# The second block of a top-2 expert folds its halves into its own accumulator banks, and its down products run by pairs of weight pieces

## The chip, the cores and the metric

One core of a Trainium2 chip runs the whole kernel as one launch. The metric is the device time of one execution in microseconds (us). The engines are TensorE (PE in the profile, with PEld for its weight loads), VectorE (DVE), ScalarE (ACT), GpSimd (POOL) and SyncE (SP), which issues most DMAs. Differences of under about 0.3% can't be told from none on this kernel.

## The reference

The layer takes x of 2048 tokens by 1024 channels. A mixer (windowed attention, a bidirectional mLSTM, two merge gates) adds to x; then a mixture of experts adds to it again:

```
h = rmsnorm(x, norm2_g)
group  = argmax(h @ w_rg + b_rg)                    # one of 4
top2   = top_k(expert logits of that group, 2)      # of 8 experts
weight = softmax(top2 values) * p_group
for each expert e (32 of them), for the tokens routed to it:
    y = (silu(xb @ w_gate[e]) * (xb @ w_up[e])) @ w_down[e]     # 1024 -> 512 -> 1024, float32
    out[token] += weight * y
```

The expert weights are 6.3 MB per expert in float32, all of which are read. The change lies in the experts alone.

## The kernel before, in words

Up to about 1744 us of the span the kernel runs the mixer and the router; from there to the end it runs a loop over the 32 experts. Every float32 operand of a large product is kept as a high and a low part in the engine's faster float32 form (`ehi`/`elo` for weights, `xhi`/`xlo` for tokens, `hhi`/`hlo` for the hidden layer), and a product is three or four matmuls of 128 rows by 512 columns.

Weights come by DMA from SP into a ring of six tiles (`raw`, `rawd`). `wsplit` cuts each tile into two pieces; ScalarE writes a piece's high part (L1572), VectorE its low part (L1573). An expert has 12 pieces: 0 to 7 for gate and up, 8 to 11 for down. The pieces of the next expert are split at named places of the present one, from a fixed table (`SPLITS`).

The tokens of an expert are handled in blocks. Block A (class `Block`) takes the first 128. Where an expert has between 129 and 192 tokens, a second block B (class `Small`) takes up to 64 more. It lays the high parts of its 64 tokens and their low parts side by side as the 128 stationary columns, so one matmul per weight part does for both (L1710); the two 64-row halves of the sum have to be added afterwards. The number of tokens is known only at run time, so B's work stands in `tc.If(v > 0)`, with A's part of the same stretch in both branches. In this data 15 of the 32 experts have a block B.

All of this stage is issued in the written order (a manual schedule), and each engine runs its own instructions in that order. The order on TensorE for an expert with a block B is:

1. A's gate and up products (L1619, L1622); B's transposes (L1704), the rest of A's, and B's gate and up products into two PSUM banks, `self.ps[0]` and `self.ps[1]` (L1710). ScalarE copies the first bank to `g[:, 0]` (L1718), VectorE the second to `g[:, 1]` (L1720).
2. `A_.after`: A's down products for pieces 0 and 1, then the transposes of A's second hidden half into A's tile `th` (`A_.p`, one PSUM bank; L1638). ScalarE reads them into `hhi` (L1639) and VectorE into `hlo` (L1640). At the place `t1` the first weight pieces of the next expert are split and its tokens transposed (`xturn`, L1596, read by L1597 and L1598).
3. `A_.end(between)`: `between(0)`, A's down products of pieces 2 and 3 for the left half (L1647, L1650), `between(1)`, the same for the right half. `between(h)` is `B_.fold(h, A_.p)`.
4. `B_.down`: B's 16 down matmuls into `self.ps[0]` and `self.ps[1]` (L1710), whose two halves ScalarE and VectorE then add with the token's weight (L1741, L1742). GpSimd adds the result to the output in DRAM (L1744).

`fold(h)` turns the 128 rows of `g[:, h]` into columns and adds the two halves in one step, with a matmul against `sel`, which holds two 64 by 64 identities on top of each other (L1726). Four such products, two matmul records each, give a 128 by 256 result in PSUM: for h = 0 in the first half of A's bank `th`, for h = 1 in its second half. Then ScalarE takes the silu of half of it (L1728), VectorE multiplies by the other half (L1729, the last read of that bank), ScalarE writes the high part (L1731) and VectorE the low part (L1732) of `hs`, the stationary operand of B's down products: fold 0 makes `hs[:, 0:2]`, fold 1 makes `hs[:, 2:4]`.

The framework places the waits. It takes two uses of the same PSUM bank as one another's to wait for, whichever columns they touch. The scopes that matter:

```
A_ = Block(...)     # th: mp.tile([P, 2, 2, P], F32, name="th"), one buffer
B_ = Small(...)     # self.ps: two banks, tags a0B and a1B
```

Of the kernel before, what the change touches and what calls it, by code (L numbers as in the profile page):

```python
# [102 lines left out]
def body(tc, A, out, scr_ext=None, upto="all"):  # L103
    nc = tc.nc
    scr_ext = scr_ext or {}
    es = ExitStack()
    with es:
        pass
        _body(tc, nc, A, out, scr_ext, upto, es)


def _body(tc, nc, A, out, scr_ext, upto, es):
# [875 lines left out]
    while pi < len(plan) and plan[pi][1] not in ("br", "wo"):  # L988
        c, kind, i = plan[pi]
# [339 lines left out]
    def put(si, ent, i, n):  # L1329
        for u in range(n):  # L1330
            nc.gpsimd.indirect_dma_start(
                out=slot_ap, out_offset=bass.IndirectOffsetOnAxis(ap=si[:, i, u:u + 1], axis=0),
                in_=ent[:, i, u, :], in_offset=None)
# [85 lines left out]
    while pi < len(plan):  # L1419
        c, kind, i = plan[pi]  # L1420
# [13 lines left out]
        if kind == "wo" and i == 0:  # L1434
            for u in range(TPC):
                t = c * TPC + u
# [139 lines left out]
    def wsplit(n):  # L1576
        if n >= NPC * N_EXP or n in wts:
            return
        wload(n // 2)
        wts[n] = split(raws[n // 2], n % NPC)  # L1580
        if n % 2:
            del raws[n // 2]
            wload(n // 2 + NRAW)

    def gather(col, tag):
        xg = mo.tile([P, D], F32, name="xg", tag="xg" + tag, bufs=2)
        nc.gpsimd.indirect_dma_start(out=xg, out_offset=None, in_=h2_ap,
                                     in_offset=bass.IndirectOffsetOnAxis(ap=col, axis=0))
        return xg

    def xturn(xg, i):

        xs = [mo.tile([P, 4, P], F32R, name=f"x{m}{i}") for m in ("hi", "lo")]
        p = mp.tile([P, 4, P], F32, name="tr", bufs=2)
        for k in range(4):
            nc.tensor.transpose(p[:, k, :], xg[:, (4 * i + k) * P:(4 * i + k + 1) * P], ident)  # L1596
        nc.scalar.activation(xs[0], p, AF.Copy)  # L1597
        nc.vector.tensor_sub(xs[1], p, xs[0].bitcast(F32))  # L1598
        return xs

    class Block:
# [40 lines left out]
        def down(self, h, ks):  # L1642
            if len(self.dn) == h:
                self.dn.append(self.ps())
            for k in ks:
                for w_ in self.wt(8 + k):
                    nc.tensor.matmul(self.dn[h], self.hhi[:, k, :], w_[:, h, :],  # L1647
                                     start=k == 0 and w_ is self.wt(8)[0], stop=False)
            for k in ks:
                nc.tensor.matmul(self.dn[h], self.hlo[:, k, :], self.wt(8 + k)[0][:, h, :], start=False, stop=k == 3)  # L1650
# [39 lines left out]
    class Small:  # L1690
# [28 lines left out]
                else:  # L1719
                    nc.vector.tensor_copy(self.g[:, 1, :], self.ps[1])  # L1720

        def fold(self, h, room):

            p = room[:, h].rearrange("p a (b t) -> p (a b) t", b=2)
            for k in range(4):
                nc.tensor.matmul(p[:, k, :], self.g[:, h, k * P:(k + 1) * P], sel, start=True, stop=True)  # L1726
            a = self.a[:, h]
            nc.scalar.activation(a, p[:, 0:2], AF.Silu)  # L1728
            nc.vector.tensor_mul(a, a, p[:, 2:4])  # L1729
            hs = self.hs[:, 2 * h:2 * h + 2]  # L1730
            nc.scalar.activation(hs[:, :, 0, :], a, AF.Copy)  # L1731
            nc.vector.tensor_sub(hs[:, :, 1, :], a, hs[:, :, 0, :].bitcast(F32))  # L1732

        def down(self):
            y = self.g[0:64].rearrange("p h f -> p (h f)")
            for k in range(4):
                for h in range(2):
                    self.product(h, self.hs, self.wt(8 + k), k, 4)
            for h in range(2):
                cs = slice(512 * h, 512 * h + 512)  # L1740
                nc.scalar.activation(y[:, cs], self.ps[h][64:128, :], AF.Copy, scale=self.wgt[64:128, :])  # L1741
                nc.vector.scalar_tensor_tensor(y[:, cs], self.ps[h][0:64, :], self.wgt[0:64, :], y[:, cs],  # L1742
                                               op0=OP.mult, op1=OP.add)
            nc.gpsimd.indirect_dma_start(out=out, out_offset=bass.IndirectOffsetOnAxis(ap=self.idx[0:64, :], axis=0),  # L1744
                                         in_=y, in_offset=None, compute_op=OP.add)
# [10 lines left out]
    def gather_small(e):  # L1756

        t = mo.tile([P, D], F32, name="xgB")
        nc.gpsimd.indirect_dma_start(out=t[0:64, :], out_offset=None, in_=h2_ap,
                                     in_offset=bass.IndirectOffsetOnAxis(ap=idx[0:64, 32 + e:33 + e], axis=0))  # L1760
        return t
# [20 lines left out]
    for e in range(N_EXP):  # L1782
        v = nc.values_load(two[:, e:e + 1], min_val=0, max_val=1)
        w_e = lambda k, e=e: wts[NPC * e + k]
        xsN = []

        def at(place):
            if place == "a1":
                if e + 1 < N_EXP:
                    xgB[e + 1] = gather_small(e + 1)  # L1790
                if e + 2 < N_EXP:
                    xg[e + 2] = gather(idx[:, e + 2:e + 3], "")
            if place == "d1" and held:
                put(*held.pop(0))
            for j in SPLITS.get(place, ()):
                wsplit(NPC * e + j)
            if place == "t1" and e + 1 < N_EXP:
                xsN.extend(xturn(xg[e + 1], i) for i in range(2))

        A_ = Block(w_e, xsA, idx[:, e:e + 1], wgt[:, e:e + 1])  # L1800
        B_ = Small(w_e, xgB[e], idx[:, 32 + e:33 + e], wg2[:, e:e + 1])
        A_.begin(at)
        with tc.If(v > 0) as cmp:
            B_.turn()
            A_.middle()
            B_.up()
        with cmp.Else():
            A_.middle()
        A_.after(at)
        with tc.If(v > 0) as cmp:  # L1810
            A_.end(lambda i: B_.fold(i, A_.p))
            B_.down()
        with cmp.Else():
            A_.end()
        at("end")
        xsA = xsN
# [44 lines left out]
```

## Time and profile before

| | |
|---|---|
| median of 3 runs | 2579.93 us (2575.63 to 2582.38) |
| profiled execution: its own time | 2579.44 us |
| its span, first to last instruction | 2577.6 us |
| granted TensorE clock, mean over the span | 0.977 of full speed |
| busy: PE, PEld, DVE, ACT, POOL | 94%, 81%, 64%, 51%, 36% |
| block B's: copies to g (L1718, L1720), folds | 15 of each copy, 30 folds |
| DMA | 515 MB, 200 GB/s in the mean |

The expert stage is the last 830 us or so of the span, the last 13 of the 40 slices of the page. A matmul record has a modelled end, and neighbouring matmuls overlap in it by design, so distances between starts are the safer measure.

### The profile page before, as it was taken

How to read it: one execution, taken by the hardware profiler on the slowest of the kernel's cores; microseconds unless marked ns; L12 is line 12 of the kernel's file. 1: busy time of each engine (PE TensorE's matmuls, PEld its weight loads, DVE VectorE, ACT ScalarE, POOL GpSimd, SP SyncE). 2: the span in 40 equal slices, each digit the busy share in tenths (PEclk: the TensorE clock that was granted, in tenths of full speed). 3: DMA queues.
4: the chain of work that ended last, by engine and by line, in shares of the span. 5: the costliest groups of instructions: out<-in, count | busy, mean ns of one | idle time of the engine just before them, and what ended most of it. 6: DMA issues, size and time to landing. Idle time of an engine off the chain costs nothing. (4 is left out here: it accounts for less than half of the span.)

```text
span 2577.6 us, 39210 instructions
## 1 busy us (share of the span) xinstructions
PE 2420.9 (94%) x13932; PEld 2090.1 (81%) x13933; DVE 1660.2 (64%) x2795; ACT 1312.2 (51%) x2564; POOL 931.0 (36%) x918
## 2 busy tenths in 40 slices
PE   7999999999999999997898889979999999999997
PEld 6889988899889989886787778867777777777776
DVE  4465455664556655578659484677866776778665
ACT  4455455464556555454342333236755665667554
POOL 5543444443543533333444445432221222122111
PEclk9999999999999999998999999989999999999999
DMA  4535434453445445556867565459998897889974
GB/s 146 162 116 169 148 109 125 144 181 94 127 138 158 134 121 163 182 174 193 244 193 209 176 180 168 131 192 322 363 318 294 255 328 235 299 255 361 343 245 103
DMA packets 348413, 515.33 MB, mean 200 GB/s; under 512 B 25019, under 2 KB 212500, under 8 KB 348188
## 3 DMA queue, kind: packets, MB, share of 16 engines
q1 hardware_dynamic: 332140, 460.03, 54.4%
q0 software_dynamic: 14880, 48.20, 8.0%
q10 hardware_dynamic: 1168, 4.21, 0.4%
q8 instruction: 127, 2.08, 0.3%
q14 instruction: 98, 0.80, 0.1%
HBM read 420.83 MB, written 91.54 MB: 199 GB/s over the span
## 5 line engine op out<-in xcount | busy, mean ns | idle before, releaser
L239 POOL TENSOR_TENSOR wlo<-wraw,whi 128x512 fp32r<-128x512 f32 (+1 forms) x422 | 574.1, 1390 | 403.2 <-ACT whi L236 386.4
L1573 DVE TENSOR_TENSOR elo<-raw,ehi 128x1024 fp32r<-128x1024 f32 x256 | 299.4, 1219 | 27.5 <-ACT ehi L1572 27.4
L319 PE MATMUL mm<-hThi,whi 128*128 128x512 f32 x768 | 306.4, 399 | 0.0
L319 PE MATMUL mm<-hTlo,whi 128*128 128x512 f32 x768 | 304.9, 397 | 0.0
L319 PE MATMUL mm<-hThi,wlo 128*128 128x512 f32 x768 | 303.6, 395 | 0.0
L236 ACT ACTIVATE whi<-wraw 128x512 fp32r<-128x512 f32 (+1 forms) x424 | 234.0, 622 | 130.0 <-PE mm L319 75.9
L319 PE MATMUL mm<-whi,hThi 128*128 128x256 f32 (+1 forms) x896 | 262.1, 292 | 3.0 <-ACT ev L908 1.8
L1572 ACT ACTIVATE ehi<-raw 128x1024 fp32r<-128x1024 f32 x256 | 254.1, 1050 | 19.7 <-DMA raw<-w_expert_up 17.8
L319 PE MATMUL mm<-wlo,hThi 128*128 128x256 f32 (+1 forms) x896 | 257.5, 287 | 1.5 <-POOL wlo L239 1.5
L319 PE MATMUL mm<-whi,hTlo 128*128 128x256 f32 (+1 forms) x896 | 258.1, 288 | 0.0
L1687 POOL DMA_INDIRECT out<-y,idx x32 | 55.4, 1731 | 448.8 <-DVE y L1686 223.2
L1619 PE MATMUL mm<-ehi,xhi 128*128 128x512 f32 x512 | 205.5, 401 | 0.0
L1619 PE MATMUL mm<-ehi,xlo 128*128 128x512 f32 x512 | 201.0, 393 | 0.4 <-DVE xlo L1598 0.4
L319 PEld LDWEIGHTS mm<-whi,hThi 128*128 128x128 f32 x896 | 172.3, 192 | 5.4 <-ACT ev L908 2.1
L319 PEld LDWEIGHTS mm<-wlo,hThi 128*128 128x128 f32 x896 | 172.4, 192 | 2.5 <-POOL wlo L239 1.8
L319 PEld LDWEIGHTS mm<-whi,hTlo 128*128 128x128 f32 x896 | 171.9, 192 | 0.9 <-DVE hTlo L449 0.2
L319 PEld LDWEIGHTS mm<-hThi,wlo 128*128 128x128 f32 x768 | 144.4, 188 | 31.1
L319 PEld LDWEIGHTS mm<-hThi,whi 128*128 128x128 f32 x768 | 144.6, 188 | 29.1
L319 PEld LDWEIGHTS mm<-hTlo,whi 128*128 128x128 f32 x768 | 144.5, 188 | 28.3
L1622 PE MATMUL mm<-elo,xhi 128*128 128x512 f32 x512 | 159.0, 392 | 0.0
L1573 DVE TENSOR_TENSOR elo<-rawd,ehi 128x1024 fp32r<-128x1024 f32 x128 | 151.4, 1220 | 11.6 <-ACT ehi L1572 11.4
L833 DVE SCALAR_TENSOR_TENSOR cacc<-cstg,colv,cacc 128x512 f32<-128x512 f32 x128 | 108.1, 845 | 58.4 <-ACT cacc L830 56.5
(456 smaller groups left out, 5932.0 us busy)
## 6 DMA issues: line engine op xcount, KB each, us to landing
wraw<-w_in SPq DMA_DIRECT2D x152, 512.0 KB, 4.3
raw<-w_expert_gate SPq DMA_DIRECT2D x128, 512.0 KB
raw<-w_expert_up SPq DMA_DIRECT2D x128, 512.0 KB, 10.1
rawd<-w_expert_down SPq DMA_DIRECT2D x64, 1024.0 KB, 12.5
mg_s<-evg SPq DMA_DIRECT2D x64, 256.0 KB, 3.8
gt<-mg_s SPq DMA_DIRECT2D x32, 512.0 KB, 6.5
wraw<-w_out SPq DMA_DIRECT2D x32, 512.0 KB, 7.3
mqk<-qk_s SPq DMA_DIRECT2D x16, 512.0 KB, 5.6
```

Of the source, the lines that this page charges most:

```text
L236: nc.scalar.activation(hi[:, ks, :W], r[:, k:k + 2, :W], AF.Copy)
L239: eng.tensor_sub(lo[:, ks, :W], r[:, k:k + 2, :W], hi[:, ks, :W].bitcast(F32))
L319: nc.tensor.matmul(o, l, r, start=st, stop=sp)
L833: nc.vector.scalar_tensor_tensor(acc, stg[:, r:r + CH], colv[:, j, r:r + 1], acc, op0=OP.mult, op1=OP.add)
L1572: nc.scalar.activation(dst[0], src, AF.Copy)
L1573: nc.vector.tensor_tensor(dst[1], src, dst[0].bitcast(F32), op=OP.subtract)
L1619: nc.tensor.matmul(self.gu[h], x_[:, k % 4, :], self.wt(k)[0][:, h, :], start=k == 0 and i == 0, stop=False)
L1622: nc.tensor.matmul(self.gu[h], self.xs[k // 4][0][:, k % 4, :], self.wt(k)[1][:, h, :], start=False, stop=k == KT - 1)
L1687: nc.gpsimd.indirect_dma_start(out=out, out_offset=bass.IndirectOffsetOnAxis(ap=self.idx, axis=0), in_=y, in_offset=None, compute_op=OP.add)
```

## The change

Three edits. `fold` takes no `room` any more: it writes its 256 columns into the first half of B's own bank `self.ps[h]`, whose gate and up sums have been copied to `g` by then, in place of A's bank `th`. The call passes no `A_.p`. And `down` runs the pieces by pairs: pieces 0 and 1 for the left half, 0 and 1 for the right, 2 and 3 for the left, 2 and 3 for the right, in place of left and right in turn for each piece.

```diff
-        def fold(self, h, room):
+        def fold(self, h):
 
-            p = room[:, h].rearrange("p a (b t) -> p (a b) t", b=2)
+            p = self.ps[h][:, 0:256].rearrange("p (k t) -> p k t", k=4)
             for k in range(4):
                 nc.tensor.matmul(p[:, k, :], self.g[:, h, k * P:(k + 1) * P], sel, start=True, stop=True)
...
         def down(self):
             y = self.g[0:64].rearrange("p h f -> p (h f)")
-            for k in range(4):
+            for k0 in (0, 2):
                 for h in range(2):
-                    self.product(h, self.hs, self.wt(8 + k), k, 4)
+                    for k in (k0, k0 + 1):
+                        self.product(h, self.hs, self.wt(8 + k), k, 4)
...
-            A_.end(lambda i: B_.fold(i, A_.p))
+            A_.end(lambda i: B_.fold(i))
```

## Rows read from the trace of the kernel before

**Rows 1.** The page: busy time by engine, and the granted clock in 40 slices.

```profile
PE 2420.9 (94%) x13932; PEld 2090.1 (81%) x13933; DVE 1660.2 (64%) x2795; ACT 1312.2 (51%) x2564; POOL 931.0 (36%) x918
...
PEclk9999999999999999998999999989999999999999
```

**Rows 2.** Windows of the expert stage: busy time of each engine, granted clock, DMA share.

```profile
core 0: us, PE busy (x) PEld busy (x) DVE busy (x) ACT busy (x) POOL busy (x), PEclk, DMA share, GB/s
...
2060.00:2290.00 230.00, 223.49 (x1086) 180.99 (x1085) 156.71 (x197) 133.75 (x195) 44.30 (x29) 1.00 0.85 280
2290.00:2430.00 140.00, 129.47 (x581) 102.37 (x580) 116.30 (x128) 99.60 (x128) 33.47 (x22) 0.98 1.01 343
```

**Rows 3.** Waits of PE in the expert stage: total us, times, longest.

```profile
PE mm L1647 <- ACT hh L1639: 14.7, 7, 4.0
PE th L1726 <- DVE hh L1640: 12.0, 15, 0.8
```

**Rows 4.** Waits of the weight loads in the same stretch.

```profile
PEld th L1726 <- ACT ehi L1572: 15.1, 15, 1.0
...
PEld th L1726 <- DVE sa L1729: 5.1, 15, 0.3
```

**Rows 5.** Timeline of PE, last block B: start, us, instruction, idle before.

```profile
2537.35 1.04 PE L1596 MATMUL tr<-ident,xg 128*128 128x128 f32 x8
2539.18 1.08 PE L1726 MATMUL th<-sel,g 128*128 128x64 f32 x8 [0.79 <-DVE hh L1640]
2540.06 0.48 PE L1647 MATMUL mm<-ehi,hh 128*128 128x512 f32 x1
...
2541.07 0.62 PE L1650 MATMUL mm<-ehi,hh 128*128 128x512 f32 x2
2541.61 1.10 PE L1726 MATMUL th<-sel,g 128*128 128x64 f32 x8
...
2544.00 0.39 PE L1710 MATMUL mm<-ehi,hs 128*128 128x512 f32 x1
2544.23 0.39 PE L1710 MATMUL mm<-elo,hs 128*128 128x512 f32 x1
```

**Rows 6.** Timeline of DVE in the same block.

```profile
2534.60 0.69 DVE L1720 COPY g<-mm 128x512 f32<-128x512 f32 x1 [6.89 <-PE mm L1710]
2535.21 3.49 DVE L1573 TENSOR_TENSOR elo<-raw,ehi 128x1024 fp32r<-128x1024 f32 x3
2538.61 0.42 DVE L1640 TENSOR_TENSOR hh<-th,hh 128x256 fp32r<-128x256 f32 x1
2538.95 1.22 DVE L1573 TENSOR_TENSOR elo<-raw,ehi 128x1024 fp32r<-128x1024 f32 x1
2540.08 1.28 DVE L1598 TENSOR_TENSOR xlo<-tr,xhi 128x512 fp32r<-128x512 f32 x2
2541.28 0.28 DVE L1729 TENSOR_TENSOR sa<-sa,th 128x128 f32<-128x128 f32 x1
2541.93 0.29 DVE L1732 TENSOR_TENSOR hs<-sa,hs 128x128 fp32r<-128x128 f32 x1 [0.38 <-ACT hs L1731]
2543.06 0.29 DVE L1729 TENSOR_TENSOR sa<-sa,th 128x128 f32<-128x128 f32 x1 [0.84 <-ACT sa L1728]
2543.73 0.29 DVE L1732 TENSOR_TENSOR hs<-sa,hs 128x128 fp32r<-128x128 f32 x1 [0.38 <-ACT hs L1731]
```

**Rows 7.** Timeline of ACT in the same block.

```profile
2530.97 0.60 ACT L1718 ACTIVATE g<-mm 128x512 f32<-128x512 f32 x1 [3.72 <-PE mm L1710]
...
2537.83 1.05 ACT L1572 ACTIVATE ehi<-raw 128x1024 fp32r<-128x1024 f32 x1
2538.77 1.08 ACT L1597 ACTIVATE xhi<-tr 128x512 fp32r<-128x512 f32 x2
2540.34 0.28 ACT L1728 ACTIVATE sa<-th 128x128 f32<-128x128 f32 x1 [0.49 <-ACT xhi L1597]
2541.59 0.31 ACT L1731 ACTIVATE hs<-sa 128x128 fp32r<-128x128 f32 x1 [0.97 <-DVE sa L1729]
```

**Rows 8.** Windows: the last block B's folds, and a stretch after a long idle.

```profile
2536.60:2544.00 7.40, 6.61 (x42) 5.45 (x41) 5.81 (x10) 3.79 (x9) 0.00 (x0) 1.00 0.00 0
2389.50:2392.90 3.40, 3.40 (x9) 2.65 (x9) 2.02 (x3) 2.77 (x4) 0.00 (x0) 0.50 1.05 396
```

## The prediction

> **What bounds the kernel now.** I read the busy shares first: TensorE is busy 94% of the span, VectorE, the next compute engine, 64%, and the granted clock is at or near full in almost every slice [rows 1]. That alone says nothing of the place of the change, so the windows of the expert stage come next. From 2060 to 2290 us, where six of eight experts have a block B, TensorE is busy 223.5 of 230 us at full clock and the DMA engines 0.85 of the time; from 2290 to 2430 us, where all experts but the last have none, TensorE is busy 129.5 of 140 us and the DMA share is 1.01 [rows 2]. So experts with a block B are bound by TensorE, and a run of experts without one by the weight loads. The change touches only the first kind. Third, the waits of TensorE: in the whole expert stage only two groups are worth naming, 14.7 us before A's products on ScalarE (seven times, in the experts short of weights) and 12.0 us before the fold on VectorE's L1640, fifteen times, at most 0.8 us each, so 0.8 in every block B [rows 3]. The weight loads add a second wait at the fold, 5.1 us in fifteen on L1729 [rows 4]. Last, the timelines of one block B on three engines show what those waits are made of [rows 5 to 7].
>
> **Where the fold waits.** After the eight transposes of the next expert's tokens TensorE stands still until 2539.18 [rows 5]. Fold 0 reads `g[:, 0]`, copied by ScalarE at 2530.97 and ready at 2531.57 [rows 7], so its operand is 7 us old. What it waits for is VectorE's L1640, which ends at 2538.61 + 0.42 = 2539.03 [rows 6]: the last reader of A's bank `th`, into whose other half the fold is to write. L1640 is late because VectorE stands behind three weight splits (3.49 us from 2535.21), which themselves stood behind L1720. Fold 1 then waits for L1729 of fold 0, which ends at 2541.28 + 0.28 = 2541.56, again the reader of the other half of the same bank; it starts at 2541.61.
>
> **The change part by part.**
>
> *Fold 0 into its own bank.* Its last reader before is L1718, over at 2531.57, so the wait on L1640 goes. The group of transposes lasts 1.04 us with 8 records of about 0.27 us, so starts are (1.04 - 0.27) / 7 = 0.11 apart, the last starts at 2538.12 and the next slot is 2538.23. From there to 2539.18 is 0.95 us; by the modelled end the idle time is 0.79 [rows 5]. These are the two ends; I take 0.9, nearer to the distance of starts. The count and the duration of the fold's matmuls stay.
>
> *Fold 1 into the other own bank.* The wait on L1729 goes. The second L1650 before it starts 0.23 after 2541.07, so the slot after it is 2541.53; the fold started at 2541.61: 0.08 us [rows 5]. The weight load shows 5.1 / 15 = 0.34 us [rows 4], but most of it lies beside the running L1650. The ends are 0.08 and 0.34, and I take 0.1, since the slot of the matmul sets the pace.
>
> *Down by pairs, and the wait that the change adds.* The 16 matmuls of `down` and their weight loads are the same in number and kind, 0.23 us apart (2544.00 to 2544.23) [rows 5]: no cost in themselves, either way. What is new is that B's right sum may not start in `ps[1]` until L1729 of fold 1 has read that bank. Before, the right product of piece 0 needed fold 0 alone. With TensorE 1.0 us ahead the first L1710 is due at 2543.0 and its weight load, some 0.23 earlier, at 2542.77. What each step finds:
>
> - `hs` of fold 0: VectorE runs without a gap from L1640 to the end of L1598, so L1729 stays at 2541.28, and L1732 still ends at 2541.93 + 0.29 = 2542.22 [rows 6]. That is 0.55 us before it is needed. Fold 0 now ends before 2539.85, when ScalarE leaves L1597, so its silu comes earlier than 2540.34 [rows 7], but nothing follows from that.
> - The right sum's first matmul is the fifth: 2543.0 + 4 x 0.23 = 2543.9. L1729 of fold 1 ended at 2543.35 before [rows 6] and would be in time even unmoved. It moves: fold 1 is over by about 2541.8, ScalarE's silu follows L1731 (over at 2541.90), L1729 follows L1732, and ends at about 2542.5. In the old order this matmul would be the third, due at 2543.46; the pairs buy 0.46 us that aren't used here.
> - `hs` of fold 1 is wanted by the ninth matmul at 2544.8; unmoved it ended at 2544.02, moved at about 2543.2.
>
> A's own products don't come to wait either: L1650 starts 1.01 us after L1647 [rows 5], so at 2538.23 + 0.88 + 1.01 = 2540.1, and L1640 is over at 2539.03. Behind the new wait stand the rest of `down` and the next expert's products; at the margins above they see nothing of it. What comes later is paced by the end of `down` (the copies out of `ps`, the next splits on ScalarE and VectorE, and through them the ring of weight tiles), and so moves with TensorE as a whole; the DMA share of 0.85 leaves room for it [rows 2].
>
> That a write waits for a reader of other columns is seen in this kernel's rows [rows 3, 4]. The Trainium skill, "PSUM — Partial Sum Buffer", section "PSUM bank collisions raise a hardware error", speaks against moving the fold to where the sums are made: it asks that engines be kept apart by bank and quadrant and not by address. By that rule the fifth matmul must wait for L1729; by addresses alone only the left quarters of the bank would matter and the sum would be the same, since the wait is met 0.55 us early even by the unmoved row. The trace agrees with the page: 5.1 us of such waits at fold 1.
>
> **The sum.** 0.9 + 0.1 = 1.0 us per block B, 15 blocks: 15 us. From the profiled execution's 2579.44 us that gives 2564.4. The median of the runs shown is 0.5 us above it, so I forecast 2564.7 us. The ends of the terms, 0.79 + 0.08 and 0.95 + 0.34, give 13 and 19 us: 2560 to 2567. The three runs of before stray by -4.3 and +2.5 us from their median, so the likeliest case alone reaches from 2557 to 2570.
>
> **The rivals.**
>
> *The wait stays, under another name.* The weight load of fold 0 is put down to ScalarE's L1572, 15.1 us in fifteen [rows 4]. If it really waits for that split, over at 2537.83 + 1.05 = 2538.88 [rows 7], fold 0 can start about 0.1 later, at 2539.0, and gains 0.2 us; with fold 1's 0.1 that is 0.3 x 15 = 4.5 us: 2575.4. For it: the row. Against it: the fold uses nothing that L1572 writes, the matmul starts 0.15 us after L1640 ends, and the label names only the last event of that engine. Chance 0.07.
>
> *VectorE becomes the bound.* The chain L1720, three splits, L1640, one split, L1598, L1729, L1732 has no idle time of note [rows 6] and does not move, while TensorE comes 1.0 us sooner. Its cover is 0.55 us. If the chain ended 1.2 us later (one more split ahead of it, 1.22), TensorE would wait 0.65 us and keep 0.35: 5 us in all, 2575. Against it: the wait at fold 0 is the same 0.8 in all fifteen blocks [rows 3], so the chain stands alike in all. Chance 0.06.
>
> *Slower: the clock falls at the fold.* After a long idle before A's products the clock was granted at 0.50, its lower level of 1.2 GHz, for 3.4 us [rows 8]; half of that, 1.7 us, is lost. If the new order (transposes and the fold's 64-column matmuls without a pause, ahead of the large products) brought this about in every block B, the loss would be 15 x 1.7 = 25.5 us against 15 gained: 2590. It decides the sign once it takes nine of the fifteen blocks. For it: this stretch holds the smallest matmuls of the stage. Against it: with 0.8 us more idle time in it, the block shown runs at 1.00 throughout [rows 8], and the change adds no idle time. Chance 0.04.
>
> **How the numbers follow.** The forecast has 0.83, the three rivals 0.07, 0.06 and 0.04. A difference of 0.3%, 7.7 us, is about what a measurement of this kernel can tell from none: faster means under 2572.2, which the forecast clears by 7 us. The forecast gives 0.82 to faster and 0.01 to no change; the first two rivals, both near 2575, give 0.04 and 0.09, since each may hold in some blocks only; the last gives 0.04 to slower. So 0.86, 0.10 and 0.04. The range of 8 in 10 begins at 2557 and goes up to 2574, to take in part of the first two rivals.
>
> **What would show it.** In the profile after: the waits of the fold on L1640 and L1729 are gone from both lists; fold 0 starts about 0.11 us after the last transpose and fold 1 0.23 after the second L1650; an expert with a block B that follows another takes 1.0 us less from one L1685 to the next; L1729 of fold 0 keeps its distance from L1720, and the first L1710 on `hs` shows no wait. The prediction is wrong if TensorE shows a new wait at L1710 on L1732 or L1729, if fold 0 still starts after L1572, if the experts without a block B grow by what the others lose, or if the granted clock falls in the blocks B.

## The result and the profile after

The changed kernel takes 2558.17 us (median of 5 runs, 2551.1 to 2561.41) against 2579.93; the ratio is 0.9911, 95% interval 0.9894 to 0.9927, that is 19 to 27 us less. Timed again later, beside some of the experiments, it came to 0.9911 once more (0.9896 to 0.9925). The direction and the place were as forecast; the gain was 1.45 times the 15 us of the sum, and the median stands 6.5 us under the forecast of 2564.7.

The page after: the span is 21.2 us shorter, and TensorE's busy time and the clock are as they were [rows 1].

```profile
span 2556.4 us, 39193 instructions
...
PE 2415.8 (95%) x13932; PEld 2090.7 (82%) x13933; DVE 1658.8 (65%) x2795; ACT 1310.1 (51%) x2564; POOL 926.1 (36%) x918
...
PEclk9999999999999999998999999989999999999999
```

The waits of PE in the expert stage, then the largest of its weight loads (total us, times, longest): nothing of the fold is left in either list [rows 3, 4].

```profile
PE mm L1647 <- ACT hh L1639: 10.1, 7, 2.6
PE th L1638 <- DVE ha L1630: 6.7, 9, 3.4
PE mm L1650 <- DVE hh L1640: 3.1, 9, 0.4
PE mm L1710 <- DVE xs L1706: 0.8, 2, 0.6
```

```profile
PEld mm L1647 <- issue: 11.7, 8, 2.8
PEld mm L1650 <- DVE hh L1640: 10.0, 15, 0.9
PEld th L1638 <- issue: 9.6, 8, 3.8
PEld tr L1704 <- PE mm L1622: 5.3, 15, 0.4
PEld mm L1710 <- DVE xs L1706: 5.3, 10, 1.0
PEld mm L1647 <- ACT hh L1639: 5.2, 15, 0.3
...
```

The wait of B's first product on the low part of its tokens (L1706) is down to two cases as well. In the kernel before it was:

```profile
PE mm L1710 <- DVE xs L1706: 2.2, 10, 0.5
```

The timeline of PE in the last block B, to compare with [rows 5]: fold 0 follows the transposes at once, and both folds last 1.00 us, no longer 1.08 and 1.10. The eight transposes start at 2517.57 and the first down product of B at 2523.00: 5.43 us, where it was 6.65 (2537.35 to 2544.00).

```profile
2517.57 1.04 PE L1596 MATMUL tr<-ident,xg 128*128 128x128 f32 x8
2518.44 1.00 PE L1726 MATMUL mm<-sel,g 128*128 128x64 f32 x8
2519.25 0.47 PE L1647 MATMUL mm<-ehi,hh 128*128 128x512 f32 x1
...
2520.26 0.62 PE L1650 MATMUL mm<-ehi,hh 128*128 128x512 f32 x2
2520.72 1.00 PE L1726 MATMUL mm<-sel,g 128*128 128x64 f32 x8
2521.53 0.48 PE L1647 MATMUL mm<-ehi,hh 128*128 128x512 f32 x1
...
2523.00 0.39 PE L1710 MATMUL mm<-ehi,hs 128*128 128x512 f32 x1
...
2526.63 0.39 PE L1619 MATMUL mm<-ehi,xhi 128*128 128x512 f32 x1
```

The timeline of DVE in the same block [rows 6]: from L1720 to the first L1729 it is 6.68 us, as before (2541.28 - 2534.60), so this chain did not move; the second L1729 follows at once and no longer waits for fold 1.

```profile
2514.82 0.69 DVE L1720 COPY g<-mm 128x512 f32<-128x512 f32 x1 [6.71 <-PE mm L1710]
...
2521.50 0.28 DVE L1729 TENSOR_TENSOR sa<-sa,mm 128x128 f32<-128x128 f32 x1
2522.15 0.29 DVE L1732 TENSOR_TENSOR hs<-sa,hs 128x128 fp32r<-128x128 f32 x1 [0.38 <-ACT hs L1731]
2522.36 0.28 DVE L1729 TENSOR_TENSOR sa<-sa,mm 128x128 f32<-128x128 f32 x1
```

The timeline of ACT around the end of `down` holds what the prediction had missed. Before, ScalarE's two copies out of the sums (L1741) stand one right behind the other, and the next expert's split (L1572) starts at 2548.71, 1.08 us after that expert's first L1619 on PE:

```profile
2547.42 1.26 ACT L1741 ACTIVATE g<-mm,wg 64x512 f32<-64x512 f32 x2 [3.15 <-PE mm L1710]
2548.71 1.06 ACT L1572 ACTIVATE ehi<-raw 128x1024 fp32r<-128x1024 f32 x1
```

```profile
2547.63 0.39 PE L1619 MATMUL mm<-ehi,xhi 128*128 128x512 f32 x1
```

After, the copies (one line further down in the changed file, L1742) stand apart: the left one is over before the right sum ends. The split starts at 2527.55, 0.92 us after the first L1619 (2526.63 above).

```profile
2518.05 1.05 ACT L1572 ACTIVATE ehi<-raw 128x1024 fp32r<-128x1024 f32 x1
...
2522.89 0.67 ACT L1685 ACTIVATE y<-mm,wgt 128x512 f32<-128x512 f32 x1
2525.98 0.69 ACT L1742 ACTIVATE g<-mm,wg 64x512 f32<-64x512 f32 x1 [2.42 <-PE mm L1710]
2526.83 0.69 ACT L1742 ACTIVATE g<-mm,wg 64x512 f32<-64x512 f32 x1 [0.17 <-PE mm L1710]
2527.55 1.06 ACT L1572 ACTIVATE ehi<-raw 128x1024 fp32r<-128x1024 f32 x1
```

The windows that answer to [rows 8], a stretch after a long idle and the last block B's folds: the clock stays full in the folds. In the expert stage the low clock appears only in experts without a block B and at the very end.

```profile
2353.00:2356.50 3.50, 2.97 (x7) 2.42 (x8) 3.35 (x5) 2.31 (x5) 0.00 (x0) 0.52 1.05 391
2516.80:2523.00 6.20, 6.20 (x42) 5.52 (x41) 5.46 (x9) 3.28 (x9) 0.00 (x0) 1.00 0.01 3
```

**A measure that the runs' scatter doesn't blur.** L1685 is ScalarE's copy of A's left sum, once in every expert, so from one L1685 to the next is one expert. Two neighbouring ones before, and one after, to go with the L1685 at 2522.89 above:

```profile
2510.64 0.67 ACT L1685 ACTIVATE y<-mm,wgt 128x512 f32<-128x512 f32 x1
2543.60 0.67 ACT L1685 ACTIVATE y<-mm,wgt 128x512 f32<-128x512 f32 x1
```

```profile
2491.33 0.67 ACT L1685 ACTIVATE y<-mm,wgt 128x512 f32<-128x512 f32 x1
```

Where both experts have a block B (nine distances, called BB below), the median is 32.96 us before and 31.56 after, and eight of the nine after lie within 0.03 us of it (the ninth is 31.81). Where the second alone has one (six, called -B) it is 29.58 and 28.60; where the first alone has one (six, called B-) 22.03 and 21.60. So the blocks B account for 9 x 1.40 + 6 x 0.98 + 6 x 0.43 = 21.1 us. The ten distances without any block B sum to 201.9 us before and to 206.9 and 202.7 in two profiles of the change: these weight-starved experts stray by microseconds from run to run and show no steady gain or loss. That the span of the profile after is 21.2 us shorter too is therefore partly chance: 1.1 us of it lies ahead of the first L1685, where nothing was changed, and from the first L1685 to the last two profiles of the change took 20.0 and 25.5 us less. The experiments below are read by the medians of BB, -B and B-.

### The profile page after: what moved, and what is told of

Same layout as the page of the kernel before. It is cut to its first block, busy times and chain, and to the rows that moved or that the text cites. A ratio compares the mean times of both kernels' runs of the same rounds, so it can differ in the third digit from the quotient of the medians.

```text
span 2556.4 us, 39193 instructions
## 1 busy us (share of the span) xinstructions
PE 2415.8 (95%) x13932; PEld 2090.7 (82%) x13933; DVE 1658.8 (65%) x2795; ACT 1310.1 (51%) x2564; POOL 926.1 (36%) x918
## 5 line engine op out<-in xcount | busy, mean ns | idle before, releaser
L1572 ACT ACTIVATE ehi<-raw 128x1024 fp32r<-128x1024 f32 x256 | 254.3, 1050 | 19.8 <-DMA raw<-w_expert_up 13.4
L1619 PE MATMUL mm<-ehi,xhi 128*128 128x512 f32 x512 | 205.4, 401 | 0.0
L1619 PE MATMUL mm<-ehi,xlo 128*128 128x512 f32 x512 | 200.9, 392 | 0.6 <-DVE xlo L1598 0.6
```

The source lines that it names most:

```text
L1572: nc.scalar.activation(dst[0], src, AF.Copy)
L1619: nc.tensor.matmul(self.gu[h], x_[:, k % 4, :], self.wt(k)[0][:, h, :], start=k == 0 and i == 0, stop=False)
```

## The experiments

**The banks without the pairs.**

```diff
-            for k0 in (0, 2):
-                for h in range(2):
-                    for k in (k0, k0 + 1):
-                        self.product(h, self.hs, self.wt(8 + k), k, 4)
+            for k in range(4):
+                for h in range(2):
+                    self.product(h, self.hs, self.wt(8 + k), k, 4)
```

> The change with the down products in their old order (left and right in turn for each piece); the folds stay in B's own banks. Theory: the banks are worth 1.21 us per block B (last transpose to first down product, 5.89 us before, 4.67 after), 18 us in all, and the pairs a further 0.15 to 0.2 us per block because the left sum ends four matmuls before the end of down instead of two, so that ScalarE's copies out of the sums, the next splits and VectorE's work behind them come earlier. So about 2561.5 us; the 0.18 us waits of B's first product on the low part of its tokens (L1706) come back where a block B follows another, and A's transposes in the expert after wait 0.33 instead of 0.20 us. Rival, pairs are free: 2558 us and those waits stay away. Rival, the pairs are what keeps the new wait out: the third down matmul stands idle on L1729 of fold 1, up to 0.5 us a block, 2565 us.

Measured: 2553.54 us, ratio 0.9931 (0.9913 to 0.9948); BB 31.73, -B 28.61, B- 21.73. Of the 1.40 us of BB the banks have 1.23 and the pairs 0.17, of the 0.43 of B- the banks 0.30 and the pairs 0.13. So 9 x 1.23 + 6 x 0.97 + 6 x 0.30 = 18.7 us belong to the banks, and 9 x 0.17 + 6 x 0.13 = 2.3 us to the pairs. The 16 products take 3.40 us from the first start to the last in both orders, so the pairs aren't needed to keep the new wait out. By the interval of its ratio alone this kernel can't be told from the change; the distances tell them apart. Its ACT timeline and waits show the mechanism: the copies are back to back, the next split 1.09 us after the first L1619 (2521.34 to 2522.43), and B's first product waits for VectorE's L1706 nine times.

```profile
2521.14 1.26 ACT L1741 ACTIVATE g<-mm,wg 64x512 f32<-64x512 f32 x2 [2.87 <-PE mm L1710]
2522.43 1.06 ACT L1572 ACTIVATE ehi<-raw 128x1024 fp32r<-128x1024 f32 x1
```

```profile
2521.34 0.39 PE L1619 MATMUL mm<-ehi,xhi 128*128 128x512 f32 x1
```

```profile
PE mm L1710 <- DVE xs L1706: 1.7, 9, 0.2
```

**The pairs without the banks.** The opposite edit, made to the kernel before.

```diff
-            for k in range(4):
+            for k0 in (0, 2):
                 for h in range(2):
-                    self.product(h, self.hs, self.wt(8 + k), k, 4)
+                    for k in (k0, k0 + 1):
+                        self.product(h, self.hs, self.wt(8 + k), k, 4)
```

> The kernel before with the down products by pairs alone; the folds stay in A's bank. Theory: the fold's waits stay (12.0 us on L1640, 5.1 us of weight loads on L1729), and the earlier copy of the left sum gains 0.15 to 0.2 us per block, 2 to 3 us: about 2577 us, with the waits of B's first product on L1706 gone. Rival, pairs are free: 2580 us and the same waits as before.

Measured: 2566.93 us beside 2572.33 for the kernel before in the same runs, ratio 0.9977 (0.9965 to 0.9988); BB 32.77, B- 21.89. BB gains 0.19 us, as the theory has it; the interval begins at 3 us, while the distances give 9 x 0.19 + 6 x 0.15 = 2.6. The fold's wait is as before, TensorE's waits on L1706 are gone, and the split follows the first L1619 by 0.91 us.

```profile
2533.84 1.08 PE L1726 MATMUL th<-sel,g 128*128 128x64 f32 x8 [0.80 <-DVE hh L1640]
...
2542.29 0.39 PE L1619 MATMUL mm<-ehi,xhi 128*128 128x512 f32 x1
```

```profile
2543.20 2.01 ACT L1572 ACTIVATE ehi<-raw 128x1024 fp32r<-128x1024 f32 x2
```

**One fold at a time in its own bank.** The target is chosen by h (1 in the first experiment, 0 in the second); the other fold goes to A's bank as before.

```diff
-            p = self.ps[h][:, 0:256].rearrange("p (k t) -> p k t", k=4)
+            if h == 1:
+                p = self.ps[h][:, 0:256].rearrange("p (k t) -> p k t", k=4)
+            else:
+                p = room[:, h].rearrange("p a (b t) -> p (a b) t", b=2)
```

> The change, but fold 0 writes into A's bank again; only fold 1 has B's own bank. Theory: fold 0 waits for L1640 as before (0.8 us idle in each of fifteen blocks), fold 1 waits for nothing; the gain is the 0.18 us of fold 1 and the 0.2 us of the pairs, 5 to 6 us: about 2574.5 us. Rival, the wait belongs to ScalarE's L1572 or to VectorE's load whatever the bank: fold 0 and the total as in the change, 2558 us.

> The change, but fold 1 writes into A's bank again; only fold 0 has B's own bank. Theory: fold 0 starts 0.11 us after the last transpose; fold 1 finds A's bank free, since L1640 has ended more than a microsecond before and fold 0 is no longer in it, so no wait is left: 2558 us as the change. Rival, A's bank costs fold 1 a wait anyhow: 0.1 to 0.3 us per block more, 2560 to 2563 us.

Measured: with fold 1 alone in its own bank 2567.5 us, ratio 0.9977 (0.9963 to 0.9991), BB 32.59; with fold 0 alone 2551.8 us, ratio 0.9910 (0.9889 to 0.9931), BB 31.56, the whole gain. Both as the theory has it. The two PE timelines (first fold 1 alone, then fold 0 alone; the line of the fold is L1729 in these files):

```profile
2524.94 1.08 PE L1729 MATMUL th<-sel,g 128*128 128x64 f32 x8 [0.80 <-DVE hh L1640]
...
2527.30 1.00 PE L1729 MATMUL mm<-sel,g 128*128 128x64 f32 x8
```

```profile
2514.05 1.00 PE L1729 MATMUL mm<-sel,g 128*128 128x64 f32 x8
...
2516.34 1.00 PE L1729 MATMUL th<-sel,g 128*128 128x64 f32 x8
```

It is the bank shared with a late reader that costs, not A's bank as such: fold 1 in `th` runs without a wait once fold 0 is out of it. With the pairs in place, moving fold 1 gives 32.77 - 32.59 = 0.18 us of BB, and moving fold 0 after it 32.59 - 31.56 = 1.03. The split holds in this order only: moving fold 0 alone gives all 1.21, so the second own bank isn't needed for the gain.

**The right sum first.**

```diff
-                for h in range(2):
+                for h in (1, 0):
                     for k in (k0, k0 + 1):
```

> The change with the right sum first in each pair, so that the left sum, which ScalarE copies first, ends last. Theory: both copies stand after the end of down, and ScalarE's next split comes 1.54 us after the next expert's first product in place of 0.91. Of this 0.63 us the next expert pays about 0.6 where it has a block B (wait of B's first product on L1706) and about 0.5 otherwise (A's transposes): 32.2 us from block B to block B, 8 to 9 us in all against the change, ratio to before 0.9945. The folds' waits stay away. Rival, the order of down only matters for waits inside down: 31.56 us and 0.991 as in the change.

Measured: 2562.56 us, ratio 0.9963 (0.9950 to 0.9976); BB 32.19, -B 28.64, B- 22.18. The distances are those expected, and the split comes 1.53 us after the first L1619 (2530.31 to 2531.84). Against the change that is 9 x 0.63 + 6 x 0.58 = 9.2 us. The expected ratio of 0.9945 was missed, upwards: the two ratios differ by 0.0052, 13 us (6 to 21 by their intervals, which holds the 9). So the order of `down` acts through the moment at which the sum that is copied first is done.

```profile
2530.56 1.26 ACT L1742 ACTIVATE g<-mm,wg 64x512 f32<-64x512 f32 x2 [3.32 <-PE mm L1710]
2531.84 1.06 ACT L1572 ACTIVATE ehi<-raw 128x1024 fp32r<-128x1024 f32 x1
```

**The whole left sum first.**

```diff
-            for k0 in (0, 2):
-                for h in range(2):
-                    for k in (k0, k0 + 1):
-                        self.product(h, self.hs, self.wt(8 + k), k, 4)
+            for h in range(2):
+                for k in range(4):
+                    self.product(h, self.hs, self.wt(8 + k), k, 4)
```

> The change with the whole left sum first (four pieces), then the whole right one. Theory: what the pairs gained is that ScalarE's copy of the left sum is out of the way when the right sum ends; in the change the second copy already waits 0.17 us for the right sum, so a still earlier left copy gains nothing: the distance from the next expert's first product to the next split on ScalarE stays 0.91 us, 31.56 us from one block B to the next, ratio to before 0.991. The fifth matmul now needs fold 1's hs, ready about 0.4 us before its weight load, so no new wait. Rival, the earlier the left copy the better: a further 0.17 us a block, 2.5 us less. Rival, the margin of fold 1 is gone: up to 0.5 us a block more at the fifth matmul.

Measured: 2552.76 us, ratio 0.9931 (0.9907 to 0.9954), an interval that holds 0.991; BB 31.56, the split 0.91 us after the first L1619, no wait at the fifth matmul. As expected, the left copy now ends a microsecond early and ScalarE stands idle for the right sum instead, 1.08 us in place of 0.17.

```profile
2518.62 0.69 ACT L1741 ACTIVATE g<-mm,wg 64x512 f32<-64x512 f32 x1 [1.51 <-PE mm L1710]
2520.39 0.69 ACT L1741 ACTIVATE g<-mm,wg 64x512 f32<-64x512 f32 x1 [1.08 <-PE mm L1710]
```

**How much cover VectorE's chain has.** The first edit moves a whole split behind A's second transposes, the second keeps back only VectorE's half of it.

```diff
-              "d0": (13,), "d1": (14,), "t1": (15,), "end": (16,)}
+              "d0": (13,), "t1": (14, 15), "end": (16,)}
```

> The change with the split of the next expert's third piece (ScalarE's and VectorE's part) moved from before A's second transposes to behind them. It puts one more VectorE split between L1640 and the fold's multiply, which tests the rival that VectorE's chain becomes the bound: in the change fold 0's hs are ready at 2522.44 and the first weight load of down is due at 2522.77, a cover of 0.33 us; the chain comes about 1.1 us later, so TensorE waits 0.6 to 0.8 us at the first down product of each block B, 9 to 12 us in all; A's wait on L1640 in the experts without block B (0.33 us, nine times) goes, 3 us back. Theory: ratio to before 0.994 to 0.995, 32.2 us from block B to block B. Rival, the chain has more cover than that: 0.990, no wait.

```diff
-        nc.vector.tensor_tensor(dst[1], src, dst[0].bitcast(F32), op=OP.subtract)
+        low = lambda: nc.vector.tensor_tensor(dst[1], src, dst[0].bitcast(F32), op=OP.subtract)
+        if later is None:
+            low()
+        else:
+            later.append(low)
...
+            if place == "t1" and low:
+                low.pop()()
             for j in SPLITS.get(place, ()):
-                wsplit(NPC * e + j)
+                wsplit(NPC * e + j, low if place == "d1" else None)
```

> The change with only VectorE's half of that split behind L1640, ScalarE's half in its old place. L1640 comes about 0.6 us earlier and the wait on it in the experts without block B (0.33 us, nine times) goes; VectorE stands idle about 0.35 us before L1640, so the fold's chain is that much later and uses up its cover, at most 0.1 us of wait per block B. Theory: 1.5 to 3 us less than the change, ratio to before 0.990; a candidate to beat both. Rival, no cover left: 0.3 us per block B more, ratio 0.9925.

Measured: the whole split 2564.48 us, ratio 0.9970 (0.9956 to 0.9985), BB 32.32; VectorE's half 2553.01 us, ratio 0.9928 (0.9912 to 0.9944), BB 31.70. In the first, the first down product starts 0.60 us later after the transposes (5.28 us after the last in place of 4.67), waiting for fold 0's `hs`; BB was met within 0.12 us. The ratio missed the expected one, upwards: the wait on L1640 went as hoped, but the first product that follows an expert without a block B now waits for its tokens' low part, and -B is 29.83, 1.23 us more than in the change.

```profile
PE mm L1619 <- DVE xlo L1598: 10.9, 17, 1.1
PE mm L1710 <- DVE hs L1732: 6.5, 15, 0.4
```

In the second, the wait on L1640 is gone, but 0.13 us of wait came up inside `down` (3.53 us from its first start to its last, not 3.40), and the stage from the first L1685 to the last took 793.4 us, where two profiles of the change have 793.1 and 787.6. By the distances (-B 29.38, B- 20.62) it differs from the change by 9 x 0.14 + 6 x 0.78 - 6 x 0.98 = 0.1 us. It was meant to beat both kernels and does not beat the change.

**The change again**, beside the last kernels.

> The changed kernel itself beside the others on the same chip: ratio 0.991, 31.56 us from block B to block B, 0.91 us from the next expert's first product to the next split.

Measured: 2549.25 us, ratio 0.9911 (0.9896 to 0.9925), BB 31.57. No kernel tried is faster than the change; the ones with fold 0 alone in its own bank and with the whole left sum first have its distances.

## Why the prediction was right, and where it was not

The place, the direction and the cause of the folds' waits were forecast rightly; the size was not. Two steps failed: the prices of the folds, which left out what a wait costs behind it, and the price of nothing for the new order of `down`.

- *What bounds*: right. All of the steady gain lies in distances that touch an expert with a block B. In the block shown TensorE is busy 6.20 of 6.20 us.
- *Fold 0, 0.9 us*: the cause is shown by the two experiments with one fold each. The start moved by 0.96 us (1.07 to 0.11 after the last transpose), at the upper end of the term, 0.95. In all fold 0 gave 1.03, since the wait also cost 0.07 behind it (below). That "the count and the duration of the fold's matmuls stay" was wrong in its second half: the folds went from 1.08 and 1.10 us to 1.00.
- *Fold 1, 0.1 us*: cause right, size too small. It gave 0.18: 0.08 at its start and 0.10 inside the fold, inside the bounds of 0.08 and 0.34. The slot of the first matmul alone does not set the pace, as the prediction had it.
- *Down by pairs, "no cost in themselves, either way"*: this step failed in its mechanism. The products do cost the same, and the new wait on L1729 costs nothing, as worked out; but the order also decides when the left sum is complete. By pairs it is done four matmuls before the end and not two, ScalarE's first copy starts 0.45 us earlier against the next expert's first product, and that expert's splits come 0.17 us sooner (0.91 after its first product, 1.08 before). That the rest "moves with TensorE as a whole" was therefore wrong: it moved 0.17 us ahead of TensorE. This removed waits of 0.18 us of the next block B on L1706, and in an expert without a block B that follows one with it, it cut the 0.33 us wait of A's transposes (L1638) to 0.20. Runs with the pairs alone, without them and with the right sum first agree on it.
- *The sum*: forecast 15.0 us; by the distances 21.1. With the pairs in place the banks gave 32.77 - 31.56 = 1.21 us of BB, so the folds were mis-sized by (1.21 - 1.0) x 15 = 3.2 us; the pairs, put at nothing, gave 2.3; 0.6 us of the difference is not split further.
- *The rivals*: the wait on ScalarE's L1572 was a label only; in the change fold 0 starts at 2518.44, while that split runs until 2519.10. VectorE's chain did not bind, with 0.33 us to spare rather than 0.55 (`hs` of fold 0 ready at 2522.44, the weight load due at 2522.77), since TensorE gained 0.2 us more; with one more split ahead of it, it did. The clock stayed at 1.00 in the folds.
- *The waits by bank*: those on L1640 and L1729 were placed by the framework. So the rows show which uses of a bank the program keeps apart, and not, as the prediction took them, that the chip needs it; no run here shows what the chip would do without these waits.

## What to carry to other kernels

Where a write waits for a reader of another part of its bank, price the wait from start to start over the whole passage, idle time and the first instructions behind it together. Reordering equal products is not neutral: ask which accumulator is complete when, who copies it, and what stands behind that copy. A one-engine bound is moved not only by what that engine waits for now, but by how early it lets the others go.

## What the runs showed of the hardware that was not expected

After a wait, the fold's first matmuls stand further apart than without one. In the block shown the eight of fold 0 and the next large product take 0.88 us from start to start before and 0.81 after (2518.44 to 2519.25); fold 1's take 0.91 and 0.81. With nothing to wait for, the first two starts lie 0.06 us apart, where they were 0.13 and 0.16. The weight loads, first before and then after, fit this: after a wait the fold's first load starts 0.03 and 0.00 us ahead of its matmul (2539.18 and 2541.61), without one 0.11 and 0.23 us ahead (2518.44 and 2520.72), beside earlier work. That this alone spaces the matmuls was not tried by itself.

```profile
2539.15 0.97 PEld L1726 LDWEIGHTS th<-sel,g 128*128 128x128 f32 x8 [1.00 <-ACT ehi L1572]
...
2541.61 0.97 PEld L1726 LDWEIGHTS th<-sel,g 128*128 128x128 f32 x8 [0.34 <-DVE sa L1729]
```

```profile
2518.33 0.97 PEld L1726 LDWEIGHTS mm<-sel,g 128*128 128x128 f32 x8
...
2520.49 1.09 PEld L1726 LDWEIGHTS mm<-sel,g 128*128 128x128 f32 x8
```

The idle time of the page (0.79 and 0 us) thus understates the two waits, worth 0.96 + 0.08 at the starts and 0.17 behind them.
